# Rotary embedding on one core: the first 2 MB of the output leave in one DMA instead of three

## The chip, the cores and the metric

One core of one Trainium2 chip. The metric is the device time of the kernel in microseconds, lower is better. The kernel before takes 318.21 us (median of 3 runs, 317.83 to 318.24).

## The reference

```python
# x: 8 x 2048 x 16 x 64 fp32, cos and sin: 2048 x 32 fp32
x_pairs = x.reshape(batch, seq_len, num_heads, head_dim // 2, 2)
x1, x2 = x_pairs[..., 0], x_pairs[..., 1]
out1 = x1 * cos - x2 * sin
out2 = x1 * sin + x2 * cos
out = np.stack([out1, out2], axis=-1).reshape(batch, seq_len, num_heads, head_dim)
```

64 MB of fp32 go in and 64 MB come out, with three operations on VectorE per element. A batch of 8 MB is one tile: 128 partitions with 16 sequence rows of 4 KB each.

## The kernel before

The GpSimd queue moves the tiles with casting DMAs (fp32 in memory, bf16 on chip). Only the first four rows of each partition of the first tile, the head, and the last four of the last tile, the tail, go through an fp32 staging tile and the SP and Activation queues, with ScalarE doing the cast.

```python
HEAD = 4
HEAD_RUNS = [(0, 1), (1, 2), (2, 4)]
TAIL = 4
...
head = stage.tile([P, HEAD, HD], fp32, name="st")
for k in range(HEAD):                                   # 4 loads of the head, SP and Activation in turn
    q = (nc.sync, nc.scalar)[k % 2]
    q.dma_start(out=head[:, k : k + 1], in_=x_t[0, :, k : k + 1])
nc.sync.dma_start(out=cos_sb, in_=cos_t)                # L90
nc.scalar.dma_start(out=sin_sb, in_=sin_t)              # L91
load(0, HEAD)                                           # GpSimd queue, 5 tiles ahead
for b in range(1, NX):
    load(b)
...
for b in range(B):
    if b == 0:
        rotate(b, 0, HEAD)
        nc.scalar.copy(out=head, in_=tiles[b][:, :HEAD])                        # L107
        for k0, k1 in HEAD_RUNS:
            nc.sync.dma_start(out=out_t[b, :, k0:k1], in_=head[:, k0:k1])       # L109
        rotate(b, HEAD, KP)
    for k0 in range(KP if b == 0 else 0, K, KP):
        rotate(b, k0, k0 + KP)
    if b < B - 1:
        store(b, HEAD if b == 0 else 0)                 # GpSimd queue
    if b >= 1 and b - 1 + NX < B:
        load(b - 1 + NX)
store(B - 1, 0, K - TAIL)
tail = stage.tile([P, TAIL, HD], fp32, name="st")
nc.scalar.copy(out=tiles[B - 2][:1, 0, :1], in_=tiles[B - 1][:1, K - 1, :1])    # L123: waits for the store of tile 6
nc.scalar.copy(out=tail, in_=tiles[B - 1][:, K - TAIL :])                       # L124
nc.sync.dma_start(out=out_t[B - 1, :, K - TAIL :], in_=tail)                    # L125
```

Each DMA signals its completion on a semaphore, a counter that an engine can wait for. The framework gives the DMAs of the SP and Activation queues eight of them in turn (107 to 112, 115 and 116 in the trace). A DMA moves as packets; here a packet holds one partition's rows, so that a DMA has 128 of them, 8 for each of the 16 DMA engines. With ten such DMAs (4 loads, cos, sin, 3 head stores, the tail) the ninth and the tenth use the first two again.

## Time and profile before

| | before |
|---|---|
| median, 3 runs | 318.21 us |
| span of the profiled run | 316.1 us |
| VectorE busy | 214.2 us (68%) |
| DMA engines, share of the span (q0 + q1 + q10) | 94.4 + 5.6 + 1.1% |
| head stores, landing after issue | 25.3, 45.5, 65.0 us |

q0 is the GpSimd queue, q1 is SP's and q10 Activation's. The prediction shows the lines on what bounds the kernel. First the span, then the SP queue's own waits (for what, us in total, times, longest), then the tail's DMA in the timeline (start, duration of the issue) and its time to landing:

```profile
span 316.1 us, 165 instructions
...
SPq L151 <- DMA out_dram<-xt: 12.1, 1, 12.1
SPq L151 <- DMA out_dram<-st: 2.9, 1, 2.9
...
299.37 0.33 SPq L125 DMA_DIRECT2D out_dram<-st  x1
...
DMA to landing us min/median/max: 15.5/15.5/15.5
```

The tail lands at 299.37 + 15.5 = 314.87 us. The span is 316.1 us, so 1.23 us pass between the landing and the end. L151 is the line of the launch: there SP waits for every DMA of the kernel, then the engines meet and the semaphores are cleared.

### The profile page before, as it was taken

The numbers are of one execution on the slowest core, as the hardware profiler recorded it, in microseconds if no ns is written. First come the engines' busy times: TensorE is split into PE (matmuls) and PEld (weight loads), VectorE is DVE, ScalarE is ACT, GpSimd is POOL, SyncE is SP. The second block draws the span as 40 slices with busy tenths as digits, with TensorE's granted clock in tenths as the row PEclk, the third lists the DMA queues.
The fourth block names the chain that finished last, engine by engine and source line by source line (L and its number), as shares of the span: only waits on it lengthen the run. The fifth ranks groups of instructions, "written<-read, shape, count | busy, mean of one in ns | idle before, by whom it ended". The sixth has DMA issues, their size and how long they took to land.

```text
span 316.1 us, 165 instructions
## 1 busy us (share of the span) xinstructions
DVE 214.2 (68%) x54; ACT 12.3 (4%) x5; POOL 8.9 (3%) x20
## 2 busy tenths in 40 slices
DVE  0000049999999999999999999999949994000000
ACT  0005004000000000000000000000000000000400
POOL 3000000000000001000000100000000000000000
DMA  9899999999999999999999999999999999999995
GB/s 267 213 265 224 222 211 253 228 224 216 232 224 223 385 435 491 398 361 232 203 398 514 282 199 199 522 406 265 228 294 406 399 506 423 398 406 506 402 427 249
DMA packets 3745, 102.25 MB, mean 323 GB/s; under 512 B 416, under 2 KB 416, under 8 KB 1440
## 3 DMA queue, kind: packets, MB, share of 16 engines
q0 software_dynamic: 2304, 95.42, 94.4%
q1 hardware_dynamic: 1008, 5.51, 5.6%
q10 hardware_dynamic: 432, 1.31, 1.1%
q14 instruction: 1, 0.01, 0.0%
HBM read 67.63 MB, written 67.11 MB: 426 GB/s over the span
## 4 chain that ended last, share of the span: by engine, by line
another core or an unknown queue 76%; DMA 13%; DVE 2%; ACT 2%; ACTq 0%; issue 0%
DMA sin_sb<-in_sin_dram 13%; ACT st L107 1%; ACT st L124 1%; DVE xt L78 1%; DVE xt L83 1%; DVE qt L77 1%; ACTq L89 0%; DVE s_tab L98 0%; DVE s_tab L99 0%; DVE c_tab L100 0%; ACTq L123 0%; ACT xt L123 0%; ACTq L124 0%; ACTq L107 0%
## 5 line engine op out<-in xcount | busy, mean ns | idle before, releaser
L77 DVE TENSOR_TENSOR qt<-xt,s_tab 128x8192 bf16<-128x8192 bf16 (+1 forms) x17 | 71.0, 4174 | 5.2 <-DMA xt<-in_x_dram 4.7
L78 DVE TENSOR_TENSOR xt<-xt,c_tab 128x8192 bf16<-128x8192 bf16 (+1 forms) x17 | 71.0, 4175 | 0.6
L83 DVE TENSOR_TENSOR xt<-xt,qt 128x8192 bf16<-128x8192 bf16 (+1 forms) x17 | 71.0, 4174 | 0.6
L98 DVE CAST s_tab<-sin_sb 128x512 bf16<-128x512 f32 x1 | 0.5, 457 | 43.7 <-DMA sin_sb<-in_sin_dram 43.7
L62 POOL DMA_DIRECT2D out_dram<-xt x8 | 4.3, 535 | 191.8 <-DVE xt L83 191.8
L123 ACT COPY xt<-xt 1x1 bf16<-1x1 bf16 x1 | 0.2, 193 | 239.9 <-DMA out_dram<-xt 239.9
L59 POOL DMA_DIRECT2D xt<-in_x_dram x8 | 4.4, 561 | 64.2 <-DMA out_dram<-xt 63.4
L107 ACT CAST st<-xt 128x4096 f32<-128x4096 bf16 x1 | 3.6, 3606 | 24.0 <-DVE xt L83 24.0
L124 ACT CAST st<-xt 128x4096 f32<-128x4096 bf16 x1 | 3.6, 3605 | 0.0
L96 ACT CAST xt<-st 128x4096 bf16<-128x4096 f32 x1 | 3.6, 3604 | 0.0
L96 ACT ACT_TABLE_LOAD x1 | 1.3, 1283 | 23.1 <-DMA st<-in_x_dram 23.1
L100 DVE CAST c_tab<-cos_sb 128x1024 bf16<-128x1024 f32 x1 | 0.7, 684 | 0.0
L99 DVE TENSOR_SCALAR s_tab<-sin_sb 128x512 bf16<-128x512 f32 x1 | 0.4, 444 | 0.0
L140 POOL MEMSET const-float32-0.0<- 128x1 f32 x1 | 0.1, 99 | 0.2 <-issue 0.2
L140 POOL MEMSET const-bfloat16-1.0<- 128x1 bf16 x1 | 0.1, 102 | 0.0
L140 POOL MEMSET const-uint8-127<- 128x1 uint8 x1 | 0.1, 100 | 0.0
L140 POOL MEMSET const-float32-1.0<- 128x1 f32 x1 | 0.1, 99 | 0.0
## 6 DMA issues: line engine op xcount, KB each, us to landing
xt<-in_x_dram POOLq DMA_DIRECT2D x7, 4096.0 KB, 57.7
out_dram<-xt POOLq DMA_DIRECT2D x2, 6144.0 KB, 48.2
xt<-in_x_dram POOLq DMA_DIRECT2D x1, 3072.0 KB, 21.9
out_dram<-st SPq DMA_DIRECT2D x1, 2048.0 KB, 15.5
st<-in_x_dram ACTq DMA_DIRECT2D x2, 512.0 KB, 13.4
st<-in_x_dram SPq DMA_DIRECT2D x2, 512.0 KB, 12.2
out_dram<-st SPq DMA_DIRECT2D x2, 512.0 KB, 35.4
out_dram<-st SPq DMA_DIRECT2D x1, 1024.0 KB, 65.0
```

The source lines that it names most:

```text
L59: nc.gpsimd.dma_start(out=tiles[b][:, k0:], in_=x_t[b, :, k0:])
L62: nc.gpsimd.dma_start(out=out_t[b, :, k0:k1], in_=tiles[b][:, k0:k1])
L77: nc.vector.tensor_tensor(out=rows(qt[:, :nk]), in0=rows(xp), in1=tab(s_tab), op=mult)
L78: nc.vector.tensor_tensor(out=rows(xp), in0=rows(xp), in1=tab(c_tab), op=mult)
L83: nc.vector.tensor_tensor(out=x3, in0=x3, in1=q_swap, op=add)
L96: nc.scalar.copy(out=tiles[0][:, :HEAD], in_=head)
L98: nc.vector.tensor_copy(out=s2[:, :, 0], in_=sin_sb)
L99: nc.vector.tensor_scalar_mul(s2[:, :, 1], sin_sb, -1.0)
L100: nc.vector.tensor_copy(out=c_tab.rearrange("p k (i j) -> p (k i) j", j=2), in_=cos_sb.to_broadcast([P, K * D2, 2]),)
L107: nc.scalar.copy(out=head, in_=tiles[b][:, :HEAD])
L124: nc.scalar.copy(out=tail, in_=tiles[B - 1][:, K - TAIL :])
L140: nc = _bacc.Bacc("TRN2", target_bir_lowering=False, num_devices=1)
```

## The change

The intent is fewer and larger transfers, and no more than eight DMAs on the SP and Activation queues, so that no completion semaphore is used twice.

```diff
-    HEAD_RUNS = [(0, 1), (1, 2), (2, 4)]
...
-                for k0, k1 in HEAD_RUNS:
-                    nc.sync.dma_start(out=out_t[b, :, k0:k1], in_=head[:, k0:k1])
+                nc.sync.dma_start(out=out_t[b, :, :HEAD], in_=head)
```

## The prediction

> **What bounds the kernel now.** I read the engine totals first, then the 40 slices, then the DMA queues, and last the waits. From the page:
>
> ```profile
> DVE 214.2 (68%) x54; ACT 12.3 (4%) x5; POOL 8.9 (3%) x20
> DVE  0000049999999999999999999999949994000000
> DMA  9899999999999999999999999999999999999995
> q0 software_dynamic: 2304, 95.42, 94.4%
> q1 hardware_dynamic: 1008, 5.51, 5.6%
> q10 hardware_dynamic: 432, 1.31, 1.1%
> HBM read 67.63 MB, written 67.11 MB: 426 GB/s over the span
> ```
>
> VectorE is busy for 68% of the span and works in the middle only. The row DMA is at 8 or 9 from the first slice to the last but one, and the three queues' shares sum to 101% of the 16 engines' span (packets overlap a little). The HBM line gives the rate: 134.7 MB in 316.1 us. The GB/s row of the page swings between 199 and 522 because a load reads fp32 and is counted at the bf16 size it writes; it shows no slack. Cut by stage (columns: stretch, its length, busy time of VectorE, ScalarE and GpSimd with instructions, clock, DMA share, GB/s):
>
> ```profile
> 0.00:45.00 45.00, 1.27 (x3) 4.89 (x2) 3.00 (x9) 1.00 0.98 234
> 45.00:122.30 77.30, 76.61 (x22) 3.61 (x1) 1.08 (x2) 1.00 1.06 277
> 122.30:295.50 173.20, 136.29 (x31) 0.00 (x0) 4.79 (x9) 1.00 1.01 362
> 295.50:316.10 20.60, 0.00 (x0) 3.76 (x2) 0.00 (x0) 1.00 0.87 369
> ```
>
> The DMA share is about 1 in each stage but the last, where the engines run out between about 310 and 315 us. So the 16 DMA engines bound the kernel from end to end. VectorE at 1.00 busy in the second stage is no bound: it only eats ahead. The waits say so:
>
> ```profile
> POOL xt L59 <- DMA out_dram<-xt: 63.4, 3, 26.4
> DVE qt L77 <- DMA xt<-in_x_dram: 4.7, 1, 4.7
> ```
>
> VectorE waits once for data, for 4.7 us near 233 us, while the store issued at 233.2 us lands only at 295.5 us: 62 us for a transfer that alone needs 19.6 us (8 packets per engine at 2.45 us, below), so some 42 us of older work stood ahead of it. What ends the kernel is that backlog, then the tail store. An order of instructions can't shorten it; only less time on the DMA engines can.
>
> **What the store of the head costs now.** It leaves ScalarE's copy at 55.6 us, and its three DMAs are issued on the SP queue from 55.66 us, within 1.3 us. The list of DMA issues gives:
>
> ```profile
> out_dram<-st SPq DMA_DIRECT2D x2, 512.0 KB, 35.4
> out_dram<-st SPq DMA_DIRECT2D x1, 1024.0 KB, 65.0
> out_dram<-st SPq DMA_DIRECT2D x1, 2048.0 KB, 15.5
> ```
>
> The last line is the tail store, with exactly the shape the new head store will have: 128 rows of 16 KB. Two windows of the DMA view give the time of one packet. First 63 to 77.5 us (nearly all 4 KB packets on q1), then 299.4 us to the end (16 KB packets, 128 of them, and 16 completion packets):
>
> ```profile
> q0 software_dynamic: 82, 2.65, 84.9%
> q1 hardware_dynamic: 81, 0.33, 6.0%
> ...
> q0 software_dynamic: 96, 3.93, 55.2%
> q1 hardware_dynamic: 144, 2.10, 29.8%
> ```
>
> A share times the window times 16 engines, over the packets: 0.060 x 14.5 x 16 / 81 = 0.172 us for 4 KB, and 0.298 x 16.7 x 16 / 128 = 0.62 us for 16 KB. The packet records taken one by one agree (median 0.172, 0.611; mean 0.620 for the latter), and give 0.333 us as mean for the 8 KB packets of the third store, 2.43 us for a load's 64 KB read and 2.45 us for a 64 KB write. Also in the first window: as many q1 packets as q0 packets, 81 to 82. Each engine takes one packet of each queue in turn, so 24 small packets per engine need 24 turns of about 2.6 us, 63 us, which is the 65.0 us of the list.
>
> **What the Trainium skill says.** Page "DMA: Bandwidth & Descriptors", section "Queues, rings and completion order": each engine goes round-robin between the queues at packet granularity. The trace agrees (81 against 82). Section "Issuing engines are not separate DMA queues": all issuers share the same 16 engines. The trace agrees: gaps between q0's packets, counted from the packet records over 60 to 120 us, sum to about 5.4 us per engine when the slight overlap elsewhere is taken off, the time of the small packets (5.4 us, below); they hide behind nothing. Section "Why small descriptors are slow (HBM only)": about 3 cycles per packet. With the 850 MHz of that page's "Specifications", 16 fewer packets per engine are an estimate of 0.06 us; the packet times above say more, so I use those. Section "Rules for kernel authors" tells one to coalesce small transfers; it doesn't promise anything where they queue behind others.
>
> **The change part by part.** No engine's order of compute changes; SP has one DMA in place of three, waiting for the same copy.
> - DMA time of the head, per engine: before, 16 x 0.172 + 8 x 0.333 = 2.75 + 2.66 = 5.42 us. After, 8 x 0.620 = 4.96 us. Saved: 0.46 us, on the bound, so it counts.
> - Completion packets: two fewer per engine at about 0.02 us: 0.04 us. The third store's take 3.66 us each, but q0 has no such gap beside them, so this is waiting and not occupancy.
> - Issue on SP: 1.3 us becomes about 0.4 us. Beside other work, worth 0: SP is idle from then until 299 us.
> - Moved: 8 turns of 2.43 + 0.62 us are 24.4 us, plus the some 5 us the first store waits for packets already taken (25.3 us to landing less 8 x 2.6 us). The head lands about 29 us after issue, near 85 us, not at 121 us. By then q1 has taken 5.0 us per engine where it now has taken about 2, so loads landing then come some 3 us later, and near 121 us all is level again.
> - The tail's path (last-but-one store's landing at 295.5 us, ScalarE's 3.6 us copy, SP's store) slides forward by the same half microsecond.
>
> Sum: 318.21 - 0.46 - 0.04 = 317.7 us.
>
> **The rivals.** (1) The fewer DMAs remove a wait for a completion semaphore used twice (ten DMAs were on the two hardware queues, now eight). For: the tail's copy is compiled with waits for three hardware DMAs, now for one. Against: it starts at 295.7 us, and the last of the three landed at 120.7 us; SP's first head store waited only for the copy. Worth 0. (2) The loads held up by the denser store starve VectorE. For: loads and store do share the engines, and q1 gets a bigger share of each turn. Against: the completion packets of loads 2 to 5 are at 42.9, 62.6, 83.2 and 104.3 us, and VectorE starts on those tiles at 72.3, 99.1, 125.9 and 152.6 us; the least slack is 29 us against 3 us. Even a 3 us VectorE delay would vanish in the 42 us backlog. Worth 0; at the very worst 321 us. (3) 16 KB rows run worse to HBM, or bunch up, next to loads than in the tail. For: the tail's packets are measured mostly after q0 had ended. Against: load packets keep 2.43 us with and without small packets beside them. A tenth worse would be 5.5 us, no gain: 318.2 us. (4) The small packets partly hide in the seams, and the whole saving vanishes: 318.2 us.
>
> **Range and chances.** The three runs spread over 0.4 us, as much as the effect. I add rivals 3 and 4 above and a larger per-packet saving (up to 1 us) below: 316.9 to 318.5 us. Faster by 2% needs 6.4 us, more than the head's store costs in all (5.4 us), so it is all but excluded: 0.005. Slower by 2% needs 6.4 us of idle DMA engines, for which I find no wait: 0.01. Same: 0.985.
>
> **What would show it right or wrong.** Right: q1 falls from 1008 to 720 packets (256 data packets and 32 completions fewer) at the same MB; the head's DMA lands 27 to 32 us after issue; its 16 KB packets take 0.61 to 0.64 us; the store of the last tile but one lands about 0.5 us before 295.5 us; VectorE's one wait stays 4 to 6 us. Wrong: 16 KB packets over 0.68 us, VectorE waiting for a load before 200 us, slices of DMA below 9 in the middle, or a time under 316.9 or over 318.5 us.

## The result, and the profile after

The changed kernel takes 318.07 us (median of 6 runs, 317.76 to 318.33) against 318.17 us (317.83 to 318.24). The ratio is 1.0000 with a 95% interval of 0.9987 to 1.0012. A ratio here is the mean time of one kernel's runs over that of the other's in the same rounds, so it is not quite the ratio of the medians quoted. The time lies in the predicted range, but half a microsecond of saving was predicted (a ratio of 0.9984, just outside the interval), and 0.1 us is seen on the medians and 0.02 us on the means, which the interval can't tell from nothing.

The page of the kernel after, its DMA row by 40 slices, the queues and two groups of instructions:

```profile
DMA  9899999898999999999999999999999999999995
q0 software_dynamic: 2304, 95.42, 94.5%
q1 hardware_dynamic: 720, 5.51, 4.4%
L76 DVE TENSOR_TENSOR qt<-xt,s_tab 128x8192 bf16<-128x8192 bf16 (+1 forms) x17 | 71.0, 4174 | 6.0 <-DMA xt<-in_x_dram 5.5
L121 ACT COPY xt<-xt 1x1 bf16<-1x1 bf16 x1 | 0.2, 194 | 240.8 <-DMA out_dram<-xt 240.8
```

q1 has 720 packets, as predicted, and VectorE's one wait is 5.5 us. But two slices in the middle of the DMA row are now at 8, where the prediction wanted none below 9. And the ScalarE copy that waits for the store of tile 6 does not start half a microsecond earlier, but 0.78 us later. The timeline, before and after:

```profile
295.58 0.19 ACT L123 COPY xt<-xt 1x1 bf16<-1x1 bf16 x1 [239.94 <-DMA out_dram<-xt]
...
296.36 0.19 ACT L121 COPY xt<-xt 1x1 bf16<-1x1 bf16 x1 [240.76 <-DMA out_dram<-xt]
```

Something has cost more than the packets saved.

The DMA view of the window 60 to 64.5 us shows where, first before, then after:

```profile
q0 software_dynamic: 36, 0.66, 67.7%
q1 hardware_dynamic: 33, 0.14, 7.6%
```

```profile
q0 software_dynamic: 31, 0.52, 69.4%
q1 hardware_dynamic: 32, 0.52, 27.5%
```

The view books a packet in the window in which it starts. Before, 0.66 MB are 20 load packets of 32 KB (the size written in bf16); the other 16 packets are completions of about 0.01 us. 0.677 x 4.5 x 16 / 20 is 2.44 us per load packet, the usual time. After, 0.52 MB are 16 load packets, one per engine: 0.694 x 4.5 x 16 / 16 = 3.12 us. Taken one by one from the packet records, all 16 took 3.15 to 3.43 us and the 128 packets of the new store 0.622 us each. Per engine that is some 0.8 us on one load packet, the one that started about when its first 16 KB packet went out, and a further 0.1 us or so on the one before it. The later turns show nothing of the sort. Such a long packet leaves the next slice without starts, which is how a slice falls to 8 although the engines were never idle.

The end of the kernel after, as before:

```profile
span 316.5 us, 162 instructions
...
SPq L149 <- DMA out_dram<-xt: 12.2, 1, 12.2
SPq L149 <- DMA out_dram<-st: 2.6, 1, 2.6
...
300.09 0.34 SPq L123 DMA_DIRECT2D out_dram<-st  x1
...
DMA to landing us min/median/max: 15.5/15.5/15.5
```

The tail lands at 315.59 us and the span is 316.5 us: 0.92 us in place of 1.23. The records of SP's waits say why. SP checks one semaphore alone and then eight pairs, about 61 ns apart. With ten DMAs the tail's semaphore is in the second pair, so six more checks follow its landing (0.37 us from that check to the last). With eight DMAs it is in the last pair, and all others have been checked while the tail was still under way. (The view rounds the landing to 0.1 us. Taken from the records of the semaphores, the end takes 1.26 us before and 0.89 us after, a difference of 0.37 us, which is six checks.)

So three terms move: packets saved, load packets lengthened, and a shorter end. The experiments take them apart.

### The profile page after: what moved, and what is told of

Same layout as the page of the kernel before. It is cut to its first block, busy times and chain, and to the rows that moved or that the text cites. A ratio compares the mean times of both kernels' runs of the same rounds, so it can differ in the third digit from the quotient of the medians.

```text
span 316.5 us, 162 instructions
## 1 busy us (share of the span) xinstructions
DVE 214.2 (68%) x54; ACT 12.2 (4%) x5; POOL 8.8 (3%) x20
## 4 chain that ended last, share of the span: by engine, by line
another core or an unknown queue 76%; DMA 13%; DVE 2%; ACT 2%; ACTq 0%; issue 0%
DMA sin_sb<-in_sin_dram 13%; ACT st L106 1%; ACT st L122 1%; DVE xt L82 1%; DVE xt L77 1%; DVE qt L76 1%; ACTq L88 0%; DVE s_tab L97 0%; DVE s_tab L98 0%; DVE c_tab L99 0%; ACTq L121 0%; ACT xt L121 0%; ACTq L106 0%
```

## The experiments

Twelve more runs were made, two of them of the kernels that were there already. All are correct but one. "Before" is timed in the same rounds on the same chip: medians of 9 runs at 317.95, 317.97 and 317.89 us in the three groups. Two kernels were executed only once ("one look" below) and have no interval. The theory changed between the groups, and the expectations show how.

**1. The changed kernel again** (no edit), 5 rounds.

> The changed kernel again, for a tighter interval and a second trace. Theory A (a first 16 KB packet lengthens one load packet on each engine by some 0.75 us, which gives back the 0.46 us saved on small packets): ratio to before 0.9995 to 1.001, and the trace again has 16 load packets of 3.1 to 3.4 us near 60 us. Rival B (the packet saving is real and only noise hid it): ratio 0.998 to 0.999, and the long packets are not there again.

317.77 us, ratio 0.9994 (0.9982 to 1.0007). The long load packets are there again, this time 2.69 to 3.12 us: 0.49 us per engine in sum, against 0.87 us in the first trace. The ratio allows both theories; the trace speaks for A, though the packets are shorter than the 3.1 to 3.4 us that A expected. The size of the loss varies from run to run.

**2. No head store.**

> The head is never stored; the result is wrong on purpose. It measures the whole cost of the head store when it leaves in one DMA. If the DMA engines bound the kernel end to end (both A and B): time falls by the engine time of the store against the changed kernel, 5.0 us for B (packets alone), 5.7 to 5.9 us for A (packets and the lengthened load packets). A rival C, in which the store is hidden in part in idle seams: less than 4 us.

```diff
-                nc.sync.dma_start(out=out_t[b, :, :HEAD], in_=head)
```

312.75 us, ratio 0.9839, result wrong. Against the changed kernel of the same group that is 5.0 us, the number of B, not of A. But the trace has the long load packets all the same, only elsewhere: near 99 us, 2.89 to 3.60 us, where the GpSimd queue's own first store begins. So the loss does not belong to the head's DMA: it comes with the first store of the kernel, whichever it is. The DMA engines bound the kernel from end to end: the head's time comes off whole.

**3. The first tile in one casting DMA.**

> No staged head store at all: the first tile leaves whole in one casting DMA of the GpSimd queue, as the other tiles do; same bytes, result right. Its head part costs 8 x (2.449 - 1.837) = 4.90 us per engine in place of 5.42 (before). Theory A: no burst beside loads, so the saving of 0.5 us is kept: 317.5 to 317.8 us, ratio to before 0.998 to 0.999. If the time is instead the same as before within 0.2 us, the sum of packet times doesn't predict time at this scale, and A loses ground too.

```diff
-                nc.scalar.copy(out=head, in_=tiles[b][:, :HEAD])
-                nc.sync.dma_start(out=out_t[b, :, :HEAD], in_=head)
...
-                store(b, HEAD if b == 0 else 0)
+                store(b)
```

317.55 us, ratio 0.9991 (0.9977 to 1.0004). The time came as expected, but not by the reason given: the trace has long load packets near 99 us here too (0.41 us per engine), and the landing of the tail to the end of the span takes 0.94 us, as with seven DMAs it should. That made me form theory E for the load packets, and later F for the end.

**4. The 8 KB rows first.**

> Three stores as before, but the 8 KB rows first, then the two of 4 KB. Asks whether a lengthened load packet belongs to the start of the burst and the packet size. Theory A: the load packets near 60 us are 0.1 to 0.3 us longer than 2.43 us on most engines, and none is longer when the 4 KB packets take over. Rival D (it belongs to the place in the stream, the last packet of one load, whatever the size): 0.7 us longer near 60 us.

```diff
-    HEAD_RUNS = [(0, 1), (1, 2), (2, 4)]
+    HEAD_RUNS = [(0, 2), (2, 3), (3, 4)]
```

318.16 us. Thirteen load packets near 60 us took 2.50 to 2.69 us: the loss grows with the size of the first packets (nothing with 4 KB, 0.1 to 0.2 us here, 0.5 to 0.8 us with 16 KB). But thirteen packets near 103 us, beside the 4 KB stores, were also 2.51 to 2.75 us. "None when the 4 KB packets take over" does not hold: the first 48 KB packets of the GpSimd queue came next there, after 8 KB had already gone. Rival D is out at 0.7 us.

**5 and 6. The head stored three times over**, by one DMA and by three. These two go together.

> The head stored three times to the same place, one DMA each time, each waiting for the one before (result right). Magnifies the change threefold together with x3_three. New theory E (after the first four runs): the first large store packets of the kernel lengthen one load packet per engine by 0.4 to 0.9 us, once per kernel, wherever they come; small packets first soften it. E: lengthened load packets near 60 us only, none when the second and third burst begin; time against before: + 3 x 4.98 - 5.42 + 0.6 = +10.1 us, against x3_three -0.6 to -1.0 us. Packets alone: -1.3 us against x3_three. Old theory A (every burst beside loads pays): -1.3 + 2 x 0.6 or so = 0 against x3_three, with lengthened packets in the second burst.

> The three stores of before, three times over, each waiting for the one to the same rows (result right). Time against before: two more heads at 5.42 us per engine, +10.8 us. If the small packets were hidden: much less.

```diff
+                for _ in range(3):
-                nc.sync.dma_start(out=out_t[b, :, :HEAD], in_=head)
+                    nc.sync.dma_start(out=out_t[b, :, :HEAD], in_=head)
```

```diff
-                for k0, k1 in HEAD_RUNS:
+                for k0, k1 in HEAD_RUNS * 3:
```

328.26 us (327.82 to 328.62) with one, 327.94 us (327.83 to 328.03) with three: 0.3 us more where 0.6 to 1.0 us less was expected. This is a miss. The traces hold E's points: in x3_one long load packets near 60 us only (2.73 to 3.05 us), none at the second and third burst, and the packets of the three heads cost 1.36 us less with one DMA (15.08 against 16.44 us). Two things stood against it. The tail of x3_one is again the tenth DMA, with 1.27 us to the end, and that of x3_three the sixteenth, with 0.84 us. And beside 4 KB packets the GpSimd queue's 64 KB write packets took 2.440 us on average in place of 2.446, 0.3 us over 48 of them: next to stores the small packets seem to be partly hidden. These terms would leave x3_three about 0.3 us longer in the profiled runs, but the two spans are level (326.0 and 326.1 us). By the packet records, its packets also overlap by 0.34 us more: from 50 to 260 us the data packets of all queues take 2.47 us per engine more than the time that passes, against 2.13 us in x3_one. The other runs of x3_one were 0.4 to 0.8 us longer than its profiled one, and no trace of them exists. That remainder stays open.

**7 and 8. The head store late**, beside stores of the GpSimd queue, by one DMA and by three.

> ScalarE's copy of the head and its one DMA wait for VectorE's end of the second tile (issue near 103 us), so the first store of the kernel is the GpSimd queue's, and the head leaves beside stores. E: load packets near 99 us are lengthened by the first store in the GpSimd queue, as without a head store, and none at the burst; against late_three -0.43 us, against before -0.4 + 0.4 = about 0. A: no lengthened packets from the burst, -0.43 us against late_three too. Noise only: no such difference.

> The same delay with the three stores of before. E: the lengthened load packets near 99 us appear here as well, because the small packets no longer come first; +0.3 to +0.8 us against before. A: no lengthened packets (the 4 KB ones did not cause any), 0 against before. Time above late_one by 0.43 us.

```diff
-                nc.scalar.copy(out=head, in_=tiles[b][:, :HEAD])
-                nc.sync.dma_start(out=out_t[b, :, :HEAD], in_=head)
...
+            if b == 1:                                # after both rotations of tile 1
+                nc.scalar.copy(out=mark, in_=tiles[1][:1, K - 1, :1])
+                nc.scalar.copy(out=head, in_=tiles[0][:, :HEAD])
+                nc.sync.dma_start(out=out_t[0, :, :HEAD], in_=head)
```

(The other has the three stores in the last line.) 317.83 us with one, ratio 0.9998 (0.9985 to 1.0010); 318.37 us with three, ratio 1.0012 (0.9999 to 1.0025). Both traces have the long load packets near 99 us. From 97.5 to 101.3 us in the trace with one DMA:

```profile
q0 software_dynamic: 18, 0.57, 89.8%
```

0.57 MB are 16 load packets and one 48 KB store packet of 1.83 us, which leaves (0.898 x 3.8 x 16 - 1.83) / 16 = 3.3 us per load packet, with no packet of the head in flight yet. In late_three the 4 KB packets no longer come first, and the loss appears there too. That is E's main point: a kernel with the same three DMAs escapes most of the loss or pays it, depending on which store comes first. One DMA is faster than three by 0.46 us on the means (0.54 on the medians), as 0.43 us was expected. But that expectation left out the end: 0.35 us of it is the shorter end (0.92 against 1.27 us). So this pair does not show the packet saving by itself.

**9. Before, with the tail's semaphore last.** Six loads of one element put the tail at place 16 of the hardware queues' DMAs.

> The kernel before with its three head stores, and six loads of one element behind them on the SP queue, so that the tail store is the 16th DMA of the hardware queues and uses the last of their eight semaphores. Theory F: at the end SP looks at the semaphores one pair after another, some 60 ns each; with ten DMAs the tail's semaphore is the second of nine checks and the rest follow its landing, with eight or sixteen it is the last. F: the time from the tail's landing to the end of the span falls from 1.23 to about 0.9 us, time -0.3 us against before (ratio 0.9985 to 0.9995), data path unchanged (no load packets lengthened near 60 us, landing of the tail as before within 0.2 us). Rival (the end differs by the number of DMAs outstanding or by chance): stays 1.2 us or grows.

```diff
+                for i in range(6):
+                    nc.sync.dma_start(out=spare[:1, i : i + 1], in_=cos_t[:1, i : i + 1])
```

317.49 us against 317.89, ratio 0.9990 (0.9977 to 1.0002), all five runs at or below the fastest of before's nine. Its page, its tail in the timeline and the landing:

```profile
span 315.7 us, 172 instructions
...
299.42 0.37 SPq L128 DMA_DIRECT2D out_dram<-st  x1
...
DMA to landing us min/median/max: 15.4/15.4/15.4
```

315.7 - 299.42 - 15.4 is 0.9 us, and the tail lands where it did. Six DMAs more, and 0.3 us faster: the end depends on the place of the tail's semaphore among the checks, not on the number of DMAs. The interval still touches 1, but the trace shows the shorter end by itself, and so does every other trace: by the semaphores' records the end takes 0.88 to 0.89 us in all eight with the tail's semaphore in the last pair and 1.25 to 1.26 us in all six with the tail as the tenth DMA. F holds; only the count in the expectation is loose (the tail's was the third of nine checks, one semaphore and eight pairs).

**10. The change, with the tail's semaphore early again.** Two loads of one element put the tail at place 10.

> The changed kernel with two loads of one element behind the head store, so that the tail is the tenth DMA and uses the second semaphore again. F: landing to end of span back at 1.2 to 1.3 us, time 0.3 us over the changed kernel, that is +0.1 to +0.3 us against before (ratio 1.000 to 1.001). It leaves the net of the data path: packets saved (-0.41) and load packets lengthened (+0.4 to +0.8).

```diff
+                for i in range(2):
+                    nc.sync.dma_start(out=spare[:1, i : i + 1], in_=cos_t[:1, i : i + 1])
```

318.37 us against 317.89, ratio 1.0013 (1.0000 to 1.0026).

```profile
span 316.6 us, 164 instructions
...
299.83 0.37 SPq L126 DMA_DIRECT2D out_dram<-st  x1
...
DMA to landing us min/median/max: 15.5/15.5/15.5
```

1.27 us to the end. With the end as it was before, one DMA in place of three is not faster but some 0.4 us slower (the interval just reaches 1), a little over the range expected. The long load packets are there (2.95 to 3.06 us, 0.67 us per engine in sum with those just before them).

**11. 4 KB first, then 12 KB, and the last semaphore.**

> Two head stores, 4 KB rows first and then 12 KB rows, with seven loads of one element so that the tail uses the last semaphore. Keeps both gains and avoids the lengthened load packets if small packets first soften them. E: packets 8 x 0.172 + 8 x 0.475 = 5.18 us (-0.24), wait -0.3, lengthened packets near 60 us 0 and at most 0.2 us at the second store: 317.4 to 317.6 us, ratio 0.998 to 0.999, the fastest of all with the result right. If large packets lengthen load packets whenever they first come: 0.4 us or more at the second store near 80 us, and time as the changed kernel.

```diff
-    HEAD_RUNS = [(0, 1), (1, 2), (2, 4)]
+    HEAD_RUNS = [(0, 1), (1, 4)]
...
+                for i in range(7):
+                    nc.sync.dma_start(out=spare[:1, i : i + 1], in_=cos_t[:1, i : i + 1])
```

317.97 us, ratio 1.0001 (0.9987 to 1.0014). The expectation failed. Near 60 us all is as before, but when the 12 KB packets come, every engine has one long load packet. From 80 to 84 us:

```profile
q0 software_dynamic: 17, 0.52, 71.5%
q1 hardware_dynamic: 32, 0.39, 23.6%
```

0.715 x 4 x 16 / 16 = 2.86 us per load packet. So 4 KB packets ahead do not spare the loss: they are merely small. It comes with the first packets of 8 KB or more, and it is smaller with 8 KB (0.1 to 0.2 us, experiment 4) than with 12 to 64 KB (0.4 to 0.9 us in sum). What follows pays little: the first 48 KB packets show nothing after 12 or 16 KB, and 0.1 to 0.2 us after 8 KB. Before, which goes from 4 over 8 to 48 KB, pays 0.1 us in all.

**12. Before, once more.**

> The kernel before once more, for a second trace. E: no load packet over 2.6 us near 60 us, 0.1 to 0.3 us on some near 101 us. F: 1.2 us from the tail's landing to the end.

318.05 us. Near 60 us only one load packet is over 2.5 us (2.51); near 101 us, ten are 2.61 to 2.81 us. 1.23 us to the end.

**The terms side by side.** All in us. Engine time per engine (the mean of 16) is from the packet records of each profiled run; "long packets" is all time over 2.432 us of load packets that start between 55 and 111 us. The sum is against the first row; the measured difference is of mean times, with before in the same rounds.

| kernel | head packets | long packets | landing to end | sum against before | measured |
|---|---|---|---|---|---|
| before | 5.39 | 0.11 | 1.23 | 0 | 0 |
| the change | 4.98 | 0.87 | 0.92 | +0.04 | -0.02 |
| the change again | 4.98 | 0.49 | 0.92 | -0.34 | -0.18 |
| after_early_wait | 4.98 | 0.67 | 1.27 | +0.19 | +0.42 |
| before_last_wait | 5.39 | 0.08 | 0.90 | -0.36 | -0.32 |
| soft_last_wait | 5.13 | 0.44 | 0.87 | -0.29 | -0.01 |
| late_one | 5.12 | 0.86 | 0.92 | +0.17 | -0.09 |
| late_three | 5.57 | 0.61 | 1.27 | +0.73 | +0.37 |
| no_head_store | 0 | 0.87 | 0.92 | -4.94 | -5.10 |
| x3_one | 15.08 | 0.46 | 1.27 | +10.08 | +10.26 |
| x3_three | 16.44 | 0.13 | 0.84 | +10.68 | +9.95 |

One trace stands beside four or five timed runs, and the long packets vary by 0.4 us between traces of the same kernel. All but one row agree within 0.4 us; x3_three is 0.7 us off, and most of that is found above. The three terms give the account of the change at the level of a few tenths, not finer.

The table sets the packets of one execution beside the times of others, and it hides something. In the traced executions themselves the tail lands 0.78, 0.27 and 0.51 us later than in the first trace of before (the change, the change again, after_early_wait; 0.18 and -0.02 us in before_again and before_last_wait), where packets and long packets give +0.35, -0.03 and +0.15 us. Two terms are missing. The small packets overlap other packets a little more: from 50 to 126 us the data packets take 0.81 us per engine more than the time that passes in all three traces with before's head stores, and 0.72 to 0.73 us in the three with one DMA. And the columns are means of 16 engines, while the kernel waits for the last: its completion of the tail comes 0.63 us after the mean of the 16 in before, and 0.94, 0.66 and 0.72 us in the three. Up to 0.2 us is left open.

## Why the prediction was right or wrong

- **What bounds the kernel: right.** Without the head store the time falls by 5.1 us against before, nearly all of the 5.4 us worked out for it.
- **Packets: right in themselves.** 128 packets of 0.622 us (0.620 predicted), 4.98 us per engine (4.96), 0.41 us less than before (0.46). The head lands 29.5 us after issue (29).
- **The step that failed is "Saved: 0.46 us, on the bound, so it counts".** On the same bound, one load packet per engine grows by about 0.5 to 0.8 us, 0.49 to 0.87 us in sum with its neighbours in three traces (0.08 to 0.15 us before). The prediction set rival 3 aside with "load packets keep 2.43 us with and without small packets beside them". That was true of the 4 KB packets that it had measured, and not of the 16 KB packets that were to come. It took the tail as the model for them, and the tail's big packets come long after the first store. Its own trace held a sign: eleven load packets of 2.51 to 2.74 us that start from 101.0 to 101.9 us, as the first 8 KB packets go out (from 100.7 us) and just before the first 48 KB ones (104.2 us).
- **Rival 1 was dismissed too early.** It asked whether the semaphores used twice cost a wait, looked at the two places where work starts, and found none. The gain was at the end, where SP checks all of them: 0.31 us by the views, 0.37 us by the semaphores' records, 0.32 us in the time of experiment 9. The intent's "eight DMAs in all" pays, but by the place of the tail's semaphore and not by the number eight: sixteen do as well.
- **The sum:** -0.41 for packets, +0.38 to +0.76 for the long ones (0.49 to 0.87 less the 0.11 that before pays), -0.31 at the end: -0.34 to +0.04 us, and -0.02 and -0.18 us were measured on the means of the two groups. In all three traces of one DMA the tail lands later than in before's first trace, by 0.3 to 0.8 us, so the data path lost and the shorter end gave it back. The prediction's 317.7 us lacked these two terms of opposite sign; that they nearly cancel, and that the range held, is luck.
- **Rival 4, small packets partly hidden: true in small.** The overlap that is lost with them is 0.08 us of the 0.46 us, not the whole saving; "they hide behind nothing" was nearly right.
- **Late loads: right.** VectorE's wait in the changed kernel is 5.5 us, no other appeared.

What stays open is the cause of the long packets. Size and order are shown: the first store packets of 8 KB or more, once per kernel, from either queue. Whether memory, the fabric or the engines themselves hold up the load is not, and neither is why it varies between runs.

## What to carry to other kernels

In a kernel bound by its DMA engines, work out a transfer change from the time of its packets, and then look at the packets of the other queue beside them, at the very sizes that are to come. Read the last microsecond too: the transfer that lands last should be the one whose semaphore is checked last. The fastest correct versions here (experiments 3 and 9, 317.5 us) gain 0.1% over before, with intervals that still touch 1, so none is proven to be worth having.

## What the Trainium skill lacked or had wrong

- "DMA: Bandwidth & Descriptors", "Why small descriptors are slow (HBM only)": about 3 cycles per packet would make 0.06 us of 16 packets (an estimate with that page's 850 MHz). The runs show 0.41 us, 26 ns per packet (5.39 against 4.98 us).
- The same page, "Rules for kernel authors", says to coalesce small transfers, and names 64 KB as the size under which one pays mostly overhead. For the most bandwidth it asks for 1 MiB or more per DMA. The three transfers here are of 512 KB, 512 KB and 1 MB, so the first rule is not tested. What the section lacks is a warning that joining transfers can gain nothing where others already keep the DMA engines busy: here the time was 0.4 us longer when the end is held equal (ratio 1.0013, 1.0000 to 1.0026).
- No page tells of the long load packets: with the first store packets of 8 KB or more, one load packet per engine takes up to 3.6 us in place of 2.43.
- No page tells that the end of a kernel depends on the place of the last DMA's semaphore (it would belong to "Runtime: NRT & Kernel Launch"): 0.9 to 1.3 us from the last landing to the end of the span, with the semaphores checked about 61 ns apart, so that the place is worth 0.3 to 0.4 us.
